# Gate projection as extra columns of a two-pair v unit with tokens stationary, and matmuls on zeros at the start

## The chip, the cores and the metric

The kernel runs on one core of a Trainium2 chip. The metric is the device time of one execution in microseconds; lower is better. Five engines work side by side, each through its own queue in order: TensorE (PE, whose weight loads the profile lists as PEld), VectorE (DVE), ScalarE (ACT), GpSimd (POOL) and SyncE (SP), which here issues nearly all DMAs. Dependences between engines are semaphores, set by a tile framework.

## The reference

One layer of a bidirectional encoder over 1280 tokens (1024 of the prompt, 256 of the sample) of width 2048. Only the first line of matrix work is touched here: one projection of the normalised input onto all column groups, among them the values v of the attention, the values of the mLSTM, and 16 mLSTM gate columns.

```python
hn = rmsnorm(x, norm_w)
proj = jnp.einsum('btd,dp->btp', hn, w_in)
na_q, na_k, na_v, na_g, ml_qk, ml_v, ml_o, ml_z, ml_gp = jnp.split(proj, cuts, axis=-1)
att = neighbourhood_attention(...na_q, na_k, na_v...) * silu(na_g)
gates = ml_gp.reshape(B, T, 2, 2, ML_HEADS) + gate_b
h = rmsnorm(bidirectional_mlstm(mq, mk, mv, gates))
mem = h * sigmoid(ml_o) * silu(ml_z)
y = rmsnorm(x + concat(att, mem) @ w_out)
```

## The kernel before

Numbers are fp32; every matmul operand is split into a high part `hi` (a rounded copy, made by ACT) and a low part `lo` (source minus `hi`, made by DVE), and each product is the sum of three matmuls: hi·hi, hi·lo, lo·hi (`split`, `split_a`, L175 to L185).

The tokens are worked on in two groups. Group A is the first 768 tokens, group B the other 512. For group A the projection runs as 2x2x2 Strassen-Winograd: two halves of the tokens (384 each), two halves of K (1024 each) and two halves of a pair of column blocks (128 columns each), so that 7 products stand for 8. The seven x operands, already summed and split, lie in SBUF for the whole phase (`xop`, L278; product 1 reads `xb`, the others `xg`). `first_tiles` (L294) builds them while it does the first four column blocks without Strassen: for each K block it loads x and weights, scales, splits and multiplies, and before its first matmul PE has nothing to do.

After that, `pair_a` (L479) does one pair of column blocks at a time, in an `order` (L615 to L618) of 34 pairs. It reads the pair's weights in four rounds of 512 KB (`ra` buffers, three of them), POOL makes the four weight sums of products 5, 6, 7 and 3 (`wt` tiles, `NWT` = 4 buffers), each of seven sources is split into a `wsa` tile (8 buffers), and PE takes the weights as the stationary and the 384 tokens as the moving operand: 168 matmuls of 384 columns for a pair. The seven products accumulate in seven of the eight PSUM banks (tags `pr` with 3 and `a` with 5) and are added up by DVE in `fold` in the last round. What remains of a pair, `finish_a` (L434), is a generator `bg`, whose steps are issued between the products of the next pair. For ten pairs (`SECOND`, L39) the four weight sums are also stored to DRAM (`sD`, L547) for group B, so a `wt` buffer is free only when that store has landed.

The v pairs (numbers `NCH` = 56 and up, eight of them) come out of this with columns on the partitions, and `finish_a` turns them by 12 PE transposes per pair (L470) before they are split (L177, L178, through `vo` tiles) and stored to `vS`. Group B's v projection, `proj_v` (L738), instead has the tokens stationary and 256 weight columns moving, and needs no transposes; in its unit 4 it appends the 16 gate columns (272 moving).

For group A the gate columns are a separate step, `gates_a` (L567), issued once behind the second pair (pair 6): it splits four sets of gate weights, runs 64 matmuls of 384 columns with the gate weights stationary (L591), and 12 small ones (L599) that add the two parts and turn the result into `gt`, the gate tile with tokens on the partitions.

`pc` tiles (5 buffers of 768 columns) hold results of pairs and the pieces of their finish. Tile tags and buffer counts are fixed; the framework's scheduler orders the instructions of each engine by its own simulated time line, with `tc.issue_after` pinning some of them. A v projection's weights lie in `w_in` as rows of 1024 numbers per K block pair, laid out by `_layout` (L1786).

Of the kernel before, what the change touches and what calls it, by code (L numbers as in the profile page):

```python
# [29 lines left out]
NRA, NWS, NWT, NPC, NPO = 3, 8, 4, 5, 6  # L30
# [5 lines left out]
LAG = 2  # L36
XFIRST = (0, 1, 8, 9, 2, 3, 10, 11, 4, 5)
# [10 lines left out]
def kernel(  # L48
# [242 lines left out]
    def wsa(name):  # L291
        return wa.tile([P, 2, 256], F32R, tag="wsa", name=name, bufs=NWS)

    def first_tiles():  # L294
# [41 lines left out]
        S.mul(mhalf[:, 15:16], ones[:, 0:1], 1.0)  # L336
        for kk in range(8):
# [96 lines left out]
    def finish_a(n1, Cn):  # L434
# [28 lines left out]
        if n1 >= NCH:  # L463
# [3 lines left out]
            for tt in range(GA // P):  # L467
# [3 lines left out]
                if tt in (1, 3):  # L471
                    vo = wa.tile([P, GA], F32R, tag="pc", name=f"{nm}vo{tt}", bufs=NPC)
                    vo = vo[:, :512].rearrange("p (a d) -> p a d", a=2)
                else:
                    vo = wa.tile([P, 2, 256], F32R, tag="vo", name=f"{nm}vo{tt}", bufs=1)
                store_v((n1 - NCH) // 2, tt * P, vo, b[:, :256])
                yield

# [88 lines left out]
    def gates_a():  # L567
        raw = wa.tile([P, 1024], F32, tag="ra", name="gAw", bufs=NRA)
        DM.dma_start(raw[:, :256], w_g)
        ab = [raw[:, :P], raw[:, P : 2 * P]]  # L570
        ext = [raw[:, 256 : 256 + P], raw[:, 384 : 384 + P]]
        V.tensor_tensor(ext[0], ab[0], ab[1], op=ALU.add)
        V.tensor_scalar(ext[1], ab[0], -1.0, None, op0=ALU.mult)
        st = []
        for i, src in enumerate((*ab, *ext)):
            t = wsa(f"gAt{i}").rearrange("p h c -> p (h c)")[:, : 8 * 32 + 96]
            G.memset(f(t), 0.0)
            tv = t[:, :256].rearrange("p (k h c) -> p k h c", h=2, c=16)
            sv = src.rearrange("p (k c) -> p k c", c=16)
            split_a(tv[:, :, 0, :], tv[:, :, 1, :], sv)  # L580
            st.append(t)
        sel = raw[0:32, 512:528]
        V.tensor_tensor(sel, ident[0:32, 0:16], ident[0:32, 16:32], op=ALU.add)
        gs = pc("gAg")
        for th, prods in enumerate((((0, 1), (1, 2)), ((2, 3), (3, 7)))):
            b = bank("a", f"gAb{th}")[:, :HALF]
            n = 0
            for w_, i in prods:
                for kk in range(8):
                    for hl_ in range(2):  # L590
                        PE.matmul(  # L591
                            b, st[w_][:, kk * 32 : kk * 32 + P], xop(i, kk, hl_),
                            start=n == 0, stop=n == 31,
                        )
                        n += 1
            V.tensor_copy(gs[0:32, th * HALF : (th + 1) * HALF], b[0:32])
        for tt in range(GA // P):
            b = bank("a", f"gAt{tt}")
            PE.matmul(b[:, :16], gs[0:32, tt * P : (tt + 1) * P], sel, start=True, stop=True)  # L599
            V.scalar_tensor_tensor(  # L600
                gt[:, tt, :], b[:, :16], rcs[0][:, tt : tt + 1], gb_sb, op0=ALU.mult, op1=ALU.add
            )

# [12 lines left out]
    rest = list(range(KT0, QK0, 2)) + list(range(OT0, NCH, 2))  # L616
    for i in range(NU):
        order += [QK0 + 2 * i, NCH + 2 * i, *rest[2 * i : 2 * i + 2]]  # L618
# [8 lines left out]
    for i, n1 in enumerate(order):  # L627
        bg = pair_a(n1, bg, second_pools if i == len(order) - 1 else None, i == 0, i == 1)
        if i == 1:
            gates_a()  # L630
# [107 lines left out]
    def proj_v(u, X):  # L738
# [8 lines left out]
        for r in range(4):  # L747
            raw = w_piece(w_in[NCH // 2 + u, r], f"v{u}_{r}")
            rawv = raw.rearrange("p (j f q c) -> p f q j c", j=2, f=2, q=2)
# [1021 lines left out]
def _layout(inputs):  # L1771
# [16 lines left out]
    )  # L1788
    gorder = [d * 8 + w_ * 4 + h for w_ in range(2) for d in range(2) for h in range(4)]
# [67 lines left out]
```

## Time and profile before

| | us |
|---|---|
| median of 3 runs (2548.97 to 2551.59) | 2550.65 |
| the profiled execution, whole | 2547.7 |
| its span, first to last instruction | 2546.0 |
| start of the first real matmul in the span | 7.01 |
| start of pair 4, the first `pair_a` | 75.6 |
| start of the gate matmuls (L591) | 138.7 |
| start of pair 56, the first v pair | 181.2 |
| end of the last `pair_a` (pair 54) | 1096.4 |

The page gives busy time per engine over the span; windows give it for a stretch; the waits say who stood still for whom. In all of them `A56b` is a PSUM bank of pair 56, `A56s` its split weights, `A56t` its POOL sums, `A56r` its raw weights, `fb`, `fw`, `fx`, `xr` tiles of the opening, and a line number that of the listing above, where a helper such as `split_a` stands for all its callers. A merged row of the time line gives start, length, engine, line, operands and count. Matmuls overlap, so that a pitch, start to start, is shorter than the duration of one.

### The profile page before, as it was taken

What the parts mean: (1) busy time and instruction counts of PE and PEld (TensorE: products, weight loads), DVE (VectorE), ACT (ScalarE), POOL (GpSimd) and SP (SyncE); (2) the same over time, 40 slices, a digit from 0 to 9 for tenths busy, and PEclk for the clock granted to TensorE, in tenths of its full rate; (3) what the DMA queues carried; (4) which work ended last, traced back from release to release, by engine and by line L of the source; (5) the groups of instructions that cost most, each with busy time, mean ns of one, the idle gap of its engine ahead of it and who ended that gap; (6) DMA issues with size and microseconds to landing.
All of it is one profiled execution on the core that took longest, in us unless ns stands there. A gap on an engine that the chain in (4) does not pass through costs nothing.

```text
span 2546.0 us, 44819 instructions
## 1 busy us (share of the span) xinstructions
PE 2527.1 (99%) x15150; PEld 2368.1 (93%) x15150; DVE 1979.3 (78%) x4049; ACT 1348.3 (53%) x3053; POOL 604.2 (24%) x895
## 2 busy tenths in 40 slices
PE   8999999999999999999999999999999999999998
PEld 8999999999999999999999899899998888888887
DVE  8768888898869798988875686776775665889696
ACT  8635545444444444465655666566665553344445
POOL 0435545444444444410000011010100103000002
PEclk9999999999999999999999999999999999999999
DMA  6556474536434343476777889888877849646227
GB/s 216 159 160 197 146 231 133 185 120 189 129 118 129 105 128 100 137 246 210 232 249 265 265 276 289 271 260 273 300 225 242 287 129 353 203 147 211 89 87 256
DMA packets 307757, 505.67 MB, mean 199 GB/s; under 512 B 48992, under 2 KB 195080, under 8 KB 307528
## 3 DMA queue, kind: packets, MB, share of 16 engines
q1 hardware_dynamic: 304424, 490.75, 59.9%
q0 software_dynamic: 2960, 11.80, 1.2%
q8 instruction: 120, 1.97, 0.3%
q14 instruction: 109, 0.89, 0.1%
q10 hardware_dynamic: 144, 0.26, 0.0%
HBM read 374.18 MB, written 128.52 MB: 197 GB/s over the span
## 4 chain that ended last, share of the span: by engine, by line
PE 85%; DMA 1%; DVE 0%; issue 0%; SPq 0%; ACT 0%; POOLq 0%; POOL 0%; ACTq 0%
PE pc L686 16%; PE po L1676 15%; PE pv L769 7%; PE A16b L286 1%; PE A40b L286 1%; PE A52b L286 1%; PE A48b L286 1%; PE A44b L286 1%; PE A20b L286 1%; PE A54b L286 1%; PE A14b L286 1%; PE A46b L286 1%; PE A22b L286 1%; PE A70b L286 1%; PE A38b L286 1%; PE A50b L286 1%
## 5 line engine op out<-in xcount | busy, mean ns | idle before, releaser
L1676 PE MATMUL po<-wo,mo 128*128 128x512 f32 (+1 forms) x1620 | 374.2, 392 | 0.0
L1676 PEld LDWEIGHTS po<-wo,mo 128*128 128x128 f32 x1620 | 303.4, 188 | 70.1
L178 DVE TENSOR_TENSOR ws<-wr,ws 128x512 fp32r<-128x512 f32 x144 | 98.2, 691 | 39.9 <-ACT ws L177 39.4
L177 ACT CAST ws<-wr 128x512 fp32r<-128x512 f32 x144 | 87.5, 617 | 66.4 <-PE pc L686 55.0
L177 ACT CAST mo<-mb 128x640 fp32r<-128x640 f32 x72 | 52.0, 726 | 111.6 <-PE po L1676 100.8
L118 POOL TENSOR_SCALAR rs<-rs 128x1 f32<-128x1 f32 x9 | 4.2, 468 | 369.8 <-DVE rs L1629 366.7
L178 DVE TENSOR_TENSOR mo<-mb,mo 128x640 fp32r<-128x640 f32 x72 | 58.6, 819 | 30.5 <-ACT mo L177 30.4
L1597 DVE TENSOR_TENSOR y<-y,po 128x512 f32<-128x512 f32 x89 | 57.1, 679 | 13.9 <-PE po L1676 13.8
L177 ACT CAST mo<-ms 128x640 fp32r<-128x640 f32 x40 | 28.9, 725 | 50.6 <-PE po L1676 32.7
L178 DVE TENSOR_TENSOR wsv<-wr_v,wsv 128x512 fp32r<-128x512 f32 x64 | 43.9, 692 | 13.3 <-ACT wsv L177 13.0
L177 ACT CAST wsv<-wr_v 128x512 fp32r<-128x512 f32 x64 | 38.9, 617 | 24.2 <-PE pv L769 12.7
L424 DVE SCALAR_TENSOR_TENSOR pcv<-pco,cw_sb,pcv 128x516 f32<-128x516 f32 x48 | 36.6, 763 | 8.8 <-ACT pcv L418 8.7
L178 DVE TENSOR_TENSOR mo<-ms,mo 128x640 fp32r<-128x640 f32 x40 | 32.7, 816 | 10.2 <-ACT mo L177 10.2
L1110 POOL MEMSET mls_0v<- 128x2 f32 x4 | 0.4, 102 | 162.8 <-DVE S_dt.float L178 137.4
L131 ACT ACTIVATE xq<-xq 128x1024 f32<-128x1024 f32 x20 | 21.2, 1060 | 31.5 <-DMA xq<-in_xtok_dram 31.5
L1611 ACT ACTIVATE jk<-y 128x512 f32<-128x512 f32 x39 | 24.5, 629 | 25.2 <-DVE y L1597 24.9
L286 PE MATMUL fb<-xg,fw 128*128 128x384 f32 x192 | 34.5, 334 | 0.0
L286 PEld LDWEIGHTS fb<-xg,fw 128*128 128x128 f32 x192 | 33.4, 188 | 0.0
L1560 DVE TENSOR_TENSOR ms<-mb,mb 128x640 f32<-128x640 f32 x40 | 32.6, 815 | 0.0
L807 DVE CUSTOM_DVE_ANT_0 nap_0st<-nap_0s,nap_0bt 128x384 f32<-128x384 f32 x32 | 17.7, 552 | 19.0 <-PE nap_0s L802 7.4
L263 DVE TENSOR_TENSOR pco<-pc,rstdb 128x512 f32<-128x512 f32 x28 | 19.1, 686 | 16.3 <-PE pc L686 16.1
L286 PE MATMUL fb<-xb,fw 128*128 128x384 f32 x96 | 23.7, 353 | 7.0 <-ACT fw L184 7.0
(2787 smaller groups left out, 8515.0 us busy)
## 6 DMA issues: line engine op xcount, KB each, us to landing
wr<-in_w_in_dram SPq DMA_DIRECT2D x72, 512.0 KB, 4.8
wr_v<-in_w_in_dram SPq DMA_DIRECT2D x32, 512.0 KB, 4.9
wb<-in_w_o_dram SPq DMA_DIRECT2D x48, 256.0 KB, 3.4
xq<-in_xtok_dram SPq DMA_DIRECT2D x20, 512.0 KB, 4.7
mb<-mx POOLq DMA_DIRECT2D x32, 320.0 KB, 7.9
y<-in_xtok_dram SPq DMA_DIRECT2D x35, 256.0 KB, 5.4
wr_wp<-in_w_o_dram SPq DMA_DIRECT2D x16, 512.0 KB, 6.7
vS<-vo SPq DMA_DIRECT2D x24, 256.0 KB, 5.1
```

Source lines behind the costliest of these rows:

```text
L131: S.activation(raw, raw, AF.Square, accum_out=ssq[g][:, t, q : q + 1])
L177: S.copy(hi, src)
L178: return V.tensor_tensor(lo, src, f(hi), op=ALU.subtract)
L263: V.tensor_tensor(o, src, rb, op=ALU.mult)
L286: PE.matmul(o, w(a_), x(b_), start=first and m == 0, stop=last and m == 2)
L424: V.scalar_tensor_tensor(dst[:, a:n], src[:, a + j - pad : n + j - pad], cw_sb[:, ct, j : j + 1], dst[:, a:n], op0=ALU.mult, op1=ALU.add,)
L686: PE.matmul(pb[j], t[j][:, wi, c : c + P], xs[xi], start=first and m == 0, stop=last and m == 2,)
L769: PE.matmul(outs[tt], xs[:, tt * P : (tt + 1) * P], t[:, wi, q * w : (q + 1) * w], start=first and m == 0 and (gates or tt % 2 == 0), stop ...
L1560: V.tensor_tensor(t, x, y_, op=op)
L1597: V.tensor_tensor(Y[p, q, tt], Y[p, q, tt], bk, op=op)
L1611: S.activation(jk, Y[p, q, tt], AF.Square, accum_out=ss[t][:, c : c + 1])
L1676: PE.matmul(bk[tt] if o is None else o, m[xi][:, tt * P : (tt + 1) * P], w[wi][:, cs], start=first and kk == 0 and j == 0, stop=last and j ...
```

## The change

The first two v pairs (56 and 58) are no longer two calls of `pair_a` but one `unit_v`, which computes 4 column blocks (512 columns) with the same seven products, x (128 tokens at a time) stationary and 256 weight columns moving. Products 1, 2, 3 and 7 get the 16 gate columns appended (272 moving); `gates_a` is removed, and `gt` is filled from the last columns of these products. 7 products x 3 token tiles x 256 columns do not fit into PSUM at once, so the unit makes three passes over K: products 1, 7, 5, then 6 and 3, then 2 and 4. Passes 1 and 2 load all of the unit's weights per K block (`whole`, rows of 256 numbers), pass 3 its second K half alone. Gated weights lie in `wide` tiles: tag `pc`, or tag `vo` with one buffer of 544 columns. Results are kept in four `pc` tiles and stored by `finish_v` without transposes, scaled by `rcs` in the split.

`NWT` falls from 4 to 3 buffers. The pair `OT0` (40) moves ahead of the unit, so that `order` becomes 4, 6, 24, 40, unit, 8, 26, 10, 12, 28, 60 and so on. The weights of the unit's two v blocks get another column order in DRAM, and `proj_v` reads it so for `u < 2`. In `first_tiles`, 15 matmuls of 384 columns on a zeroed tile go ahead of the first real matmul, into the bank `pb[7]`, which the first real matmul there overwrites.

```diff
-NRA, NWS, NWT, NPC, NPO = 3, 8, 4, 5, 6
+NRA, NWS, NWT, NPC, NPO = 3, 8, 3, 5, 6
+WARM = 15
...
         S.mul(mhalf[:, 15:16], ones[:, 0:1], 1.0)
+        idle = pc("idle")[:, :HALF].bitcast(F32R)
+        V.memset(f(idle), 0.0)
+        for i in range(WARM):
+            PE.matmul(pb[7], idle[:, :P], idle, start=True, stop=True)
...
+    def wide(name, i):
+        if i % 2:
+            return wa.tile([P, GA], F32R, tag="pc", name=name, bufs=NPC)[:, :544]
+        return wa.tile([P, 544], F32R, tag="vo", name=name, bufs=1)
+
+    def finish_v(u, z, C):
+        for tt in range(3):
+            t = 3 * z + tt
+            vo = wide(f"V{u}o{t}", tt % 2)[:, :512].rearrange("p (a d) -> p a d", a=2)
+            store_v(u, t * P, vo, C[:, tt * 256 : (tt + 1) * 256], rcs[0][:, t : t + 1])
+            yield
...
+    def unit_v(u, bg, gw):
...
+        def weights(i, kk, src):
+            gated = i in (1, 2, 3, 7)
+            if gated:
+                t = wide(f"{nm}s{kk}{i}", i == 1 or i in (2, 3) and kk % 2 == 0)
+                t = t.rearrange("p (h c) -> p h c", h=2)
+            else:
+                t = wsa(f"{nm}s{kk}{i}")
+            hi = S.copy(t[:, 0, :256], src)
+            lo = V.tensor_tensor(t[:, 1, :256], src, f(t[:, 0, :256]), op=ALU.subtract)
+            last_split["ins"] = lo.ins
+            if gated:
+                with tc.issue_after(hi.ins), tc.issue_after(lo.ins):
+                    split(t[:, 0, 256:], t[:, 1, 256:], gw[:, i == 2, kk], -1.0 if i == 7 else None)
+            splits[i, kk] = t, hi.ins, lo.ins
+
+        def multiply(i, kk, b):
+            t = splits[i, kk][0]
+            w = 272 if i in (1, 2, 3, 7) else 256
+            for tt, (o, own, closes) in enumerate(b[i][0]):
+                for m, (xi, wi) in enumerate(((0, 0), (0, 1), (1, 0))):
+                    PE.matmul(
+                        o, xop(i, kk, xi)[:, tt * P : (tt + 1) * P], t[:, wi, :w],
+                        start=kk == 0 and own and m == 0, stop=kk == 7 and closes and m == 2,
+                    )
...
+        def source(i, kk, A, src):
+            if i == 1:
+                return A[0, 0]
+            t = wa.tile([P, 256], F32, tag="wt", name=f"{nm}t{kk}{i}", bufs=NWT)
+            if i == 5:
+                G.tensor_tensor(t, A[1, 0], A[1, 1], op=ALU.add)
+            elif i == 6:
+                G.tensor_tensor(t, src[5], A[0, 0], op=ALU.subtract)
+            elif i == 7:
+                G.tensor_tensor(t, A[0, 0], A[1, 0], op=ALU.subtract)
+            elif i == 3:
+                V.tensor_tensor(t, A[0, 1], src[6], op=ALU.subtract)
+            return t
...
+        def first(i, kk, b):
+            if kk < 7:
+                if i in (5, 7):
+                    next(bg, None)
+            elif i == 1:
...
+                for c, o in b[1][1]:
+                    S.copy(C[0][:, c], o)
+                gate(1, b)
+            elif i == 7:
+                new(2)
+                gate(7, b)
+                plus(2, 0, 7, b)
+            else:
+                new(3)
+                new(1)
+                plus(3, 2, 5, b)
+                plus(1, 0, 5, b)
...
+        def second(i, kk, b):
+            if kk == 7 and i == 6:
+                for h in range(2):
+                    for q in (1, 2, 3):
+                        plus(q, q, 6, b, slice(h, h + 1))
+            elif kk == 7:
+                gate(3, b)
+                plus(1, 1, 3, b)
+                scaled_gates(1)
+
+        def third(i, kk, b):
+            if kk == 7:
+                if i == 2:
+                    gate(2, b)
+                    scaled_gates(0)
+                plus(i - 2, i - 2, i, b)
+
+        def steps():
+            b = {1: place(1, ("pr",) * 3), 7: place(7, ("a",) * 3), 5: place(5, "a", "a")}
+            for kk in range(8):
+                A = whole(kk, "r")
+                for i in (1, 7, 5):
+                    yield i, kk, b, source(i, kk, A, None), first
+            b = {6: place(6, "pr", "a"), 3: place(3, ("pr", "pr", "a"))}
...
+            b = {2: place(2, ("a",) * 3), 4: place(4, "pr", "a")}
...
+        for step in chain(steps(), (None,)):
+            if step is not None:
+                weights(step[0], step[1], step[3])
+            if todo is not None:
+                i, kk, b, _, after = todo
+                multiply(i, kk, b)
+                with ExitStack() as es:
+                    if step is not None and kk == 7:
+                        for ins in splits[step[0], step[1]][1:]:
+                            es.enter_context(tc.issue_after(ins))
+                    after(i, kk, b)
+            todo = step
+        return chain(*(finish_v(u + q // 2, q % 2, C[q]) for q in (1, 3, 0, 2)))
...
-    def gates_a():
...
+        if n1 == NCH:
+            bg = unit_v(0, bg, gw)
+        else:
+            bg = pair_a(n1, bg, second_pools if i == len(order) - 1 else None, i == 0, i == 1)
         if i == 1:
-            gates_a()
+            gw = wa.tile([P, 2, 8, 16], F32, tag="gw", name="gw", bufs=1)
+            DM.dma_start(gw, w_g.rearrange("p (f k c) -> p f k c", f=2, c=16))
...
+            if u < 2:
+                rawv = raw.rearrange("p (f q j c) -> p f q j c", f=2, q=2, j=2)
+            else:
+                rawv = raw.rearrange("p (j f q c) -> p f q j c", j=2, f=2, q=2)
...
+    vw = w_in[NCH // 2 : NCH // 2 + 2].reshape(2, 4, P, 2, 2, 2, P).transpose(0, 1, 2, 4, 5, 3, 6)
+    w_in[NCH // 2 : NCH // 2 + 2] = vw.reshape(2, 4, P, 1024)
```

More of the change, by code (lines that the diff above doesn't have):

```diff
@@ L565, in pair_a @@
         return finish_a(n1, Cn)
-    def gates_a():
[L568 to L602, printed above, removed]
     opening = first_tiles()
```

74 lines of the change are left out of this document (68 added, 6 removed).

## The prediction

> **What bounds the kernel now.** First the head of the page and the windows of the two halves: TensorE (PE) is busy nearly all the time.
>
> ```profile
> span 2546.0 us, 44819 instructions
> PE 2527.1 (99%) x15150; PEld 2368.1 (93%) x15150; DVE 1979.3 (78%) x4049; ACT 1348.3 (53%) x3053; POOL 604.2 (24%) x895
> 40.00:1096.00 1056.00, 1054.09 (x6092) 1048.61 (x6091) 881.63 (x1599) 517.94 (x1230) 492.10 (x552) 1.00 0.48 150
> PE fb L286 <- ACT fw L184: 7.0, 1, 7.0
> PE A4b L286 <- DVE A4s L185: 0.8, 3, 0.3
> ```
>
> In a window's row the length comes first, then busy time and count of PE, PEld, DVE, ACT and POOL, then clock and DMA share. From 40 to 1096 us, where the change lies, PE idles 1.9 us of 1056, and the waits (last two rows: total, times, longest) hold only the 7.0 us before the first matmul and trifles. So in this part time is the sum of PE's matmul pitches; whatever leaves PE is saved, as long as the other engines keep up.
>
> Next the places that the diff touches: a v pair (A56), the pair behind a v pair, in which its 12 transposes run (A40), one with neither (A10), the gate matmuls (three windows), and the two pairs around them.
>
> ```profile
> 181.21:210.31 29.10, 29.10 (x169) 29.10 (x169) 28.81 (x46) 15.15 (x35) 15.03 (x15) 1.00 0.40 119
> 682.87:713.27 30.40, 30.40 (x180) 30.23 (x180) 26.22 (x51) 13.65 (x36) 14.49 (x18) 1.00 0.41 138
> 240.80:270.10 29.30, 29.30 (x171) 29.26 (x170) 22.95 (x45) 14.67 (x36) 18.05 (x16) 1.00 0.72 230
> 138.72:149.96 11.24, 11.24 (x66) 10.99 (x65) 7.60 (x17) 3.28 (x8) 2.75 (x4) 1.00 0.51 141
> 149.96:150.72 0.76, 0.76 (x7) 0.73 (x6) 0.66 (x3) 0.41 (x1) 0.00 (x0) 1.00 1.08 344
> 154.27:155.04 0.77, 0.77 (x7) 0.74 (x7) 0.34 (x2) 0.34 (x1) 0.71 (x1) 1.00 0.61 189
> 108.80:138.72 29.92, 29.57 (x169) 29.11 (x169) 26.85 (x55) 17.18 (x43) 14.68 (x19) 1.00 0.71 209
> 150.72:181.20 30.48, 30.48 (x175) 30.20 (x175) 17.56 (x40) 11.35 (x28) 11.06 (x15) 1.00 0.47 140
> ```
>
> **Removed: the gate matmuls.** 64 matmuls of 384 columns and 12 small ones took 11.24 + 0.76 + 0.77 = 12.77 us of PE. Upper bound: the pairs around them last 29.92 and 30.48 - 0.77 = 29.71 against 29.10, so up to 1.43 us more may hang on the gates. I take 12.8; the neighbours have other reasons too (the 0.8 us of waits at A4 are of this kind).
>
> **Two v pairs against one unit.** The two pairs cost 2 x 29.10 = 58.20 us for 336 matmuls of 384 columns (0.1732 each). The unit has 7 products x 8 K blocks x 3 token tiles x 3 hi/lo terms = 504 matmuls: 288 of 272 columns (products 1, 2, 3, 7) and 216 of 256. The second half's v projection already runs both widths, its x (tokens) stationary; its line alone gives:
>
> ```profile
> 1096.56:1100.28 3.72, 3.72 (x30) 3.72 (x31) 1.00 0.97 323
> 1837.41:1839.99 2.58, 2.58 (x22) 2.54 (x22) 1.00 1.01 371
> ```
>
> That is 0.1240 us for 272 columns and 0.1173 us for 256. The unit: 288 x 0.1240 + 216 x 0.1173 = 61.05 us, 2.85 more than the pairs, gates included. The weight loads, one for each matmul, are hidden at both pitches.
>
> The Trainium skill (TensorE: Matmul & The Clock Gate, "Back-to-back issue gap") gives sustained spacings of about 81 ns for 128 columns and 131 ns for 512, a large fixed part; an estimate on that line is 98 ns for 256, 100 for 272 and 114 for 384, hence 49.9 us for the unit against 38.4 for the pairs, 11.5 more instead of 2.85. This rule speaks against many short matmuls; the trace disagrees: from 256 to 384 columns the pitch grows by 56.0 ns of 173.2, so the fixed part is only 0.1173 - 2 x 0.0560 = 5 ns.
>
> **Removed: 24 transposes.** The trace shows two between matmuls:
>
> ```profile
> 692.22 0.38 PE L470 MATMUL A64v<-ident,A64c 128*128 128x128 f32 x2
> 692.36 4.79 PE L286 MATMUL A40b<-xg,A40s 128*128 128x384 f32 x26
> ```
>
> 0.14 us for two is 0.84 for 12, the lower bound; the pair with them lasts 30.40 - 29.30 = 1.10 us longer than A10, and 1.30 longer than A56, the upper bound. I take 1.1, as it holds the breaks around them: 2.2 us for both pairs (1.7 to 2.6).
>
> **Matmuls on zeros.** The first matmuls run slowly:
>
> ```profile
> 7.00:11.00 4.00, 3.99 (x12) 1.00 1.01 307
> 11.00:15.00 4.00, 4.00 (x24) 1.00 1.09 349
> 12.01 0.40 ACT L184 CAST fw<-fr 128x256 fp32r<-128x256 f32 x1
> 12.13 0.96 DVE L185 TENSOR_TENSOR xg<-xr,xg 128x768 fp32r<-128x768 f32 x1 [2.73 <-ACT xg L184]
> 13.12 0.68 PE L286 MATMUL fb<-xg,fw 128*128 128x384 f32 x3
> ```
>
> 12 in 4.00 us, then 24 in 4.00, though the clock column says 1.00 in both. 15 on zeros last 15 x 0.333 = 5.0 us; DVE and PE have nothing before 4.8 and 7.01 us, so they delay nothing. But the second half of the first K block starts at 13.12 and its operands are complete at 12.41 (ACT) and 13.09 (DVE). A faster first half can start it 0.7 us earlier at most, and then waits for DVE. I take 0.3 us (0 to 0.7).
>
> The Trainium skill (the same page, "What's actually happening") says that the array runs at half clock until some 3.4 us of activity; the doubling agrees. By this rule alone 12 slow matmuls would be worth 12 x 0.167 = 2.0 us, and the sum 1.7 us lower; it leaves out when the operands come.
>
> PE alone: -12.8 + 2.85 - 2.2 - 0.3 = **-12.4 us**.
>
> **What feeds the unit.** For each step ACT and DVE make a hi/lo split, as before (56 of them), plus 32 small ones for gate columns; POOL's 32 sums stay as many, and DVE gets 8 sums (product 3) that POOL made before.
>
> ```profile
> L185 DVE TENSOR_TENSOR A56s<-A56t,A56s 128x256 fp32r<-128x256 f32 x13 | 6.9, 537 | 0.0
> L185 DVE TENSOR_TENSOR A56s<-A56r,A56s 128x256 fp32r<-128x256 f32 x9 | 5.9, 654 | 0.0
> L185 DVE TENSOR_TENSOR A56s<-A56t,A56s x16: 408/412/959, 176.0 to 206.8; 128x256 fp32r<-128x256 f32 x16
> 152.21 0.23 DVE L600 SCALAR_TENSOR_TENSOR gt<-gAt,rstdc,gb_sb 128x16 f32<-128x16 f32 x1
> L1597 DVE TENSOR_TENSOR y<-y,po 128x512 f32<-128x512 f32 x89 | 57.1, 679 | 13.9 <-PE po L1676 13.8
> ```
>
> A split takes 0.412 us in the median, up to 0.959, and 0.585 on average here ((13 x 0.537 + 9 x 0.654) / 22). DVE's work in the unit: 56 x 0.585 + 32 x 0.23 + 8 x 0.585 = 44.8, and to empty PSUM 15 pieces of 256 columns (0.41), 6 of 512 (0.68) and 12 of 16 (0.23) = 13.0; in all 57.8 us under 61.05 of PE. DVE fits, with 3 us to spare, but the emptying comes in lumps. At the end of pass 1 the last product's four additions (2 x 0.68 + 2 x 0.41 = 2.2 us) have the next product's 9 x 0.117 = 1.06 to hide in: 1.1 us late, with product 3's sum and split queued behind them on DVE and PE waiting for these. At the end of pass 2 product 6's six additions take 3.3 us against 1.1: 2.2 us late if pass 3's first splits stand behind. Splits put ahead hide some of it: I take **+2.5 us** (0 to 3.3).
>
> **wt from 4 to 3 buffers.** POOL already waits here, for DVE's splits or, in the ten pairs that spill their sums, for the spill to land:
>
> ```profile
> POOL A10t L531 <- DMA sD<-A10t: 6.3, 3, 3.0
> DMA to landing us min/median/max: 2.1/3.6/4.6
> 260.83 0.43 DVE L185 TENSOR_TENSOR A10s<-A10r,A10s 128x256 fp32r<-128x256 f32 x1 [4.45 <-ACT A10s L184]
> L286 PE MATMUL A10b<-xb,A10s x24: 331/335/342, 240.8 to 263.7; 128*128 128x384 f32 x24
> ```
>
> A10's last round has its first split ready at 261.3 us and its first matmul (five pitches before 263.7) at 262.8: 1.5 us of cover in the worst spilling pair, up to eight splits of about 1 us elsewhere. With three buffers a sum waits for the spill one sum later, about 1 us. That stays under the cover: I take **+0.5 us**, with 0 and 10 x 1.1 = 11 as ends.
>
> The sum: -12.4 + 2.5 + 0.5 = -9.4, so 2547.7 - 9.4 = 2538.3 us for a run like the profiled one. The median shown (2550.65) is 2.95 above it: **2541 us**, with its own range 2538 to 2545.
>
> **Rivals.**
> (a) Nothing stalls and the upper bounds hold: -14.2 + 2.85 - 2.6 - 0.7 = -14.7, 2536 us. For it: eight splits of cover today and DVE below PE; against: passes that must empty banks.
> (b) The three wt buffers: each spilling pair loses 1.1 us: -12.4 + 2.5 + 11 = +1.1, 2552 us. For it: A10's 1.5 us of cover; against: it is the worst one.
> (c) The raw weights come too late. Passes 1 and 2 each read all 4 MB of the unit, pass 3 half, in rows of 1 KB where a pair reads 4 KB rows.
>
> ```profile
> A56r<-in_w_in_dram SPq DMA_DIRECT2D x4, 512.0 KB, 3.5
> fr<-in_w_in_dram SPq DMA_DIRECT2D x16, 256.0 KB, 6.3
> ```
>
> With the opening's 6.3 us (512-byte rows) and 3.5 us from landing to the last reader, three buffers give a K block per 9.8 / 3 = 3.27 us; pass 1 takes 3.4 on PE, pass 2 only 2.17: 8 x 1.1 = 8.8 us. -12.4 + 8.8 = -3.6, 2547 us. Against: at 3.5 us the ring gives 2.33.
> (d) Slower: DVE becomes the bound of the unit, every split at 0.959 as beside a running POOL sum: 64 x 0.959 + 7.4 + 13.0 = 81.8 us against 61.05, +20.7; -12.4 + 20.7 = +8.3, 2559 us. It decides from a mean split of 0.63 us on ((61.05 - 20.4) / 64); slower than before from 0.83. For it: 0.585 is near; against: that average already holds POOL's sums at the same rate.
> (e) The change does not do what it says: product 7's weights have a single buffer, so PE runs alone between refills. A refill (ACT 0.41, DVE up to 0.96, two small ones) is under the 2.17 us of the two products between; this would only add to (d).
>
> **How the numbers follow.** Forecast 0.50, (a) 0.24, (b) 0.08, (c) 0.08, (d) with (e) 0.10. A measurement tells 0.2%, 5.1 us, from no change: faster is below 2545.5, slower above 2555.8. Faster 0.50 + 0.24 + a quarter of (c) = 0.76; slower is (d), 0.10; the rest 0.14. The range reaches from below (a) to (b): 2534 to 2552; outside are (d), half of (b) and a little of (a).
>
> **What would show it.** The gate matmuls gone and the pairs around at 29.1 to 29.3 us; the unit's 504 matmuls within 61 us plus gaps; those gaps at its two pass ends, with DVE as releaser; full pitch from the first real matmul, but its second half still waiting for DVE near 13 us; spilling pairs no longer than 29.3. Wrong: gaps at every K block (DMA as releaser is (c), DVE with splits near 0.96 is (d)), or POOL waits on spills that reach PE (b).

## The result, and the profile after

| | before | after |
|---|---|---|
| median of 10 runs each, us | 2550.15 (2547.94 to 2551.59) | 2556.19 (2552.14 to 2559.32) |
| ratio, 95% interval | | 1.0022 [1.0014, 1.003] |
| profiled execution: span, granted clock | 2546.0, 0.999 | 2552.1, 0.998 |
| first half ends (last matmul of pair 54) | 1096.75 | 1102.85 |
| from there to the end of the span | 1449.25 | 1449.25 |

The changed kernel is slower, by 6 us or 0.22%: the wrong sign, and outside the range. In the two profiles the whole of it lies in the first half. The head of the page after says that PE has a little less work, although 5.1 us of matmuls on zeros are now in it, and that the time went into gaps:

```profile
span 2552.1 us, 45095 instructions
PE 2525.1 (99%) x15233; PEld 2362.4 (93%) x15233; DVE 1985.9 (78%) x4087; ACT 1346.7 (53%) x3088; POOL 595.4 (23%) x891
L534 PE MATMUL V0b<-V0s,xg 128*128 128x272 f32 (+1 forms) x360 | 54.3, 295 | 8.0 <-DVE A40c L679 3.8
```

PE's sum fell by 2.0 us (from 2527.1) and the span grew by 6.1. The costliest group that is new, the unit's matmuls on `xg`, stood still for 8.0 us. To find where, the first half is cut at the first matmul of each pair. The windows of the changed kernel for pair 6 (where the gates were), pair 24, the unit, and the two pairs behind it, 8 and 26:

```profile
107.10:137.00 29.90, 29.52 (x171) 29.17 (x170) 28.01 (x55) 17.89 (x43) 15.15 (x15) 1.00 0.78 233
137.00:166.10 29.10, 29.10 (x170) 29.10 (x169) 23.14 (x43) 12.93 (x33) 15.19 (x18) 1.00 0.59 182
195.20:269.70 74.50, 65.89 (x499) 63.33 (x498) 47.02 (x130) 28.30 (x99) 22.25 (x29) 0.98 0.51 162
269.70:301.40 31.70, 30.86 (x175) 30.15 (x176) 24.04 (x50) 15.97 (x42) 14.36 (x18) 1.00 0.76 218
301.40:334.40 33.00, 30.00 (x170) 29.13 (x170) 28.84 (x54) 17.16 (x42) 18.18 (x20) 1.00 0.64 196
```

The same cuts before gave 41.9 for pair 6, 30.5 for pair 24, 58.3 for the two v pairs, 30.5 for pair 8 and 29.1 for pair 26. So the 6.1 us are:

| where | before | after | difference |
|---|---|---|---|
| start of pair 4, and pair 4 | 75.6, 33.2 | 74.5, 32.6 | -1.7 |
| pair 6 and pair 24 (gates gone) | 72.4 | 59.0 | -13.4 |
| two v pairs, then the unit | 58.3 | 74.5 | +16.2 |
| pair 8 | 30.5 | 31.7 | +1.2 |
| pair 26 | 29.1 | 33.0 | +3.9 |
| all other pairs | | | -0.1 |

A few of the unit's last matmuls are issued behind the next pair's first one: pair 8's window shows x175 where a pair alone shows x169 to x171. With these five (0.12 us each) the unit takes 75.1 us and the two pairs behind it 64.1. By pitches alone it is 61.05 for the unit, and 29.3 + 29.1 = 58.4 for two such pairs: the unit lost 14.0 us, and the pairs behind it 5.7. Against the forecast sum of -9.4 the profiles show +6.1; of these 15.5 us, 11.5 lie in the unit (2.5 were allowed for) and 5.7 behind it, and the other terms give back about 2. In the unit's window DVE is busy for 47.02 of 74.50, ACT for 28.30, and POOL for 22.25: no engine is full. The waits of PE from 190 to 335 us (total, times, longest) name several releasers, none of them large:

```profile
PE V0b L534 <- DVE A40c L679: 3.8, 2, 2.0
PE V0b L534 <- ACT V0s L178: 2.8, 3, 1.4
PE A26b L287 <- DVE A8c L679: 2.6, 2, 1.5
PE A8b L287 <- ACT A8s L185: 1.3, 2, 0.7
PE V0b L534 <- ACT V0s L181: 0.6, 1, 0.6
PE V0b L534 <- DVE V0s L179: 0.5, 1, 0.5
PE A26b L287 <- DVE A26s L186: 0.4, 1, 0.4
PE V0b L534 <- DVE V0s L182: 0.4, 1, 0.4
```

The first is the unit's beginning. PE's time line there (start, length, operation, count, idle before it):

```profile
195.21 0.54 PE L534 MATMUL V0b<-V0s,xg 128*128 128x272 f32 x3
197.77 0.65 PE L534 MATMUL V0b<-V0s,xg 128*128 128x272 f32 x3 [2.02 <-DVE A40c L679]
200.15 0.64 PE L534 MATMUL V0b<-V0s,xg 128*128 128x272 f32 x3 [1.74 <-DVE A40c L679]
201.12 4.08 PE L534 MATMUL V0b<-V0s,xg 128*128 128x256 f32 x21
```

Three matmuls, a wait, three, a wait. The banks they need are those of pair 40, which DVE is still adding up. DVE's time line shows why it is late:

```profile
193.26 1.49 DVE L435 SCALAR_TENSOR_TENSOR A24cv<-A24c,A24cv 128x766 f32<-128x766 f32 x1
...
196.83 0.43 DVE L522 TENSOR_TENSOR V0s<-V0t,V0s 128x256 fp32r<-128x256 f32 x1 [1.28 <-ACT V0s L521]
197.17 1.60 DVE L679 TENSOR_TENSOR A40c<-A40c,A40b 128x384 f32<-128x384 f32 x3
198.69 0.95 DVE L182 SCALAR_TENSOR_TENSOR A24c<-A24cv,A24ch 128x766 f32<-128x766 f32 x1
199.55 1.01 DVE L679 TENSOR_TENSOR A40c<-A40c,A40b 128x384 f32<-128x384 f32 x2
```

Before and between the additions of pair 40 stands the finish of pair 24, a convolution with pieces of 1.49 and 0.95 us. The convolution is not alone there: ahead of the additions DVE also stood idle for 1.28 us, for ACT's half of one of the unit's own splits. ACT waited for POOL's sum, and POOL had waited 0.84 us for the piece of 1.49. An ordinary pair needs the last banks of its predecessor only from its fifth product on; the unit needs three `a` banks in its first steps. After the waits, 21 matmuls take 4.08 us, 0.19 each, and the next ones 0.117 again; windows of that stretch show what this is:

```profile
201.12:204.54 3.42, 3.42 (x19) 3.42 (x18) 3.42 (x12) 1.93 (x6) 0.00 (x0) 0.54 0.35 118
204.54:205.03 0.49, 0.49 (x6) 0.49 (x5) 0.05 (x1) 0.49 (x1) 0.00 (x0) 1.00 0.06 19
```

The granted clock fell to half for one stretch of 3.4 us, so the gaps cost 1.7 us a second time. The waits in the unit (8.0 us) and this make 9.7 of the 14.0; most of the rest lies in restarts behind the waits, 0.16 us each, and in pitches that are a little longer, which were not traced further.

Behind the unit its 12 finishing tiles go to DRAM. ACT's rows from the time line at its end and in pair 26:

```profile
264.55 1.06 ACT L132 ACTIVATE xq<-xq 128x1024 f32<-128x1024 f32 x1 [3.63 <-DMA xq<-in_xtok_dram]
...
303.58 0.51 ACT L181 ACTIVATE V0o<-V0c,rstdc 128x256 fp32r<-128x256 f32 x1 [3.44 <-DMA vS<-V0o]
```

ACT works in order. Here it stood 3.63 us for an x load of the second half, with the unit's last splits behind it (PE then waits 1.44 us), and 3.44 us for the store of an earlier `V0o` tile, since the `vo` tag has one buffer. DVE's half of that tile waits for ACT's with the additions of pair 8 behind it, and PE waits for those banks (`A8c`, 2.6 us in the list).

### The profile page after: what moved, and what is told of

Read it like the earlier page. It is cut to its first block, busy times and chain, and to the rows that moved or that the text cites. A ratio compares the mean times of both kernels' runs of the same rounds, so it can differ in the third digit from the quotient of the medians.

```text
span 2552.1 us, 45095 instructions
## 1 busy us (share of the span) xinstructions
PE 2525.1 (99%) x15233; PEld 2362.4 (93%) x15233; DVE 1985.9 (78%) x4087; ACT 1346.7 (53%) x3088; POOL 595.4 (23%) x891
## 4 chain that ended last, share of the span: by engine, by line
PE 80%; DMA 1%; DVE 0%; issue 0%; ACT 0%; POOL 0%; SPq 0%; POOLq 0%; DVEq 0%; ACTq 0%
PE pc L840 16%; PE po L1833 15%; PE pv L926 6%; PE A48b L287 1%; PE A52b L287 1%; PE A22b L287 1%; PE A18b L287 1%; PE A44b L287 1%; PE A46b L287 1%; PE A54b L287 1%; PE A50b L287 1%; PE A42b L287 1%; PE A70b L287 1%; PE A68b L287 1%; PE A34b L287 1%; PE A64b L287 1%
## 5 line engine op out<-in xcount | busy, mean ns | idle before, releaser
L179 DVE TENSOR_TENSOR mo<-mb,mo 128x640 fp32r<-128x640 f32 x72 | 58.7, 824 | 31.5 <-ACT mo L178 31.4
L534 PE MATMUL V0b<-V0s,xg 128*128 128x272 f32 (+1 forms) x360 | 54.3, 295 | 8.0 <-DVE A40c L679 3.8
L534 PEld LDWEIGHTS V0b<-V0s,xg 128*128 128x128 f32 x360 | 48.7, 195 | 10.4 <-DVE A40c L679 4.2
L287 PE MATMUL fb<-xg,fw 128*128 128x384 f32 x192 | 34.7, 335 | 0.7 <-ACT xg L185 0.7
```

What stands on the lines that cost most here:

```text
L179: return V.tensor_tensor(lo, src, f(hi), op=ALU.subtract)
L287: PE.matmul(o, w(a_), x(b_), start=first and m == 0, stop=last and m == 2)
L534: PE.matmul(o, xop(i, kk, xi)[:, tt * P : (tt + 1) * P], t[:, wi, :w], start=kk == 0 and own and m == 0, stop=kk == 7 and closes and m == 2,)
```

## The experiments

All ratios are to the kernel before on the same chip, with a 95% interval. Lengths of pairs come from one profile each. The opening up to the end of pair 4, whose instructions are the same in after, `a_order` and `a_plain`, took between 105.5 and 107.1 us in these three, so differences of single profiles under about 1.5 us are not read, unless they come back in several. A unit "with all its matmuls" is its length from its first matmul to the next pair's first, and 0.12 us more for each matmul that the next pair's window shows beyond 170; the next pair is shortened by as much.

**`b_warm`, `b_wt3`: the small parts alone.** The kernel before, with the matmuls on zeros, or with three `wt` buffers.

```diff
+        idle = pc("idle")[:, :HALF].bitcast(F32R)
+        V.memset(f(idle), 0.0)
+        for i in range(15):
+            PE.matmul(pb[7], idle[:, :P], idle, start=True, stop=True)
```

> The kernel before with the 15 matmuls on zeros alone. In the changed kernel the second half of the first K block starts 1.2 us earlier (11.90 against 13.12 us). If that is the matmuls' doing: first pair 1.1 us earlier (about 74.5 us instead of 75.6), time 1 us below before. If the earlier operands of that execution did it: within 0.3 us of before.

> The kernel before with three wt buffers instead of four, nothing else. Rival (the buffer count costs the ten spilling pairs): those pairs 1 us longer each, the whole +5 to +11 us. Main theory (the loss sits around the unit): every pair within 0.3 us of before, the whole within 2 us.

`b_warm`: 1.0001 [0.9992, 1.0011]; in its profile pair 4 starts at 75.2 (before 75.6) and ends at 107.3 (108.8), and the half ends at 1094.85 (1096.75). Pair 4 thus starts 0.4 us earlier, not the 1.1 expected. The 1.5 us at its end are at the edge of what is read here, and too little for ten runs to show. `b_wt3`: 0.9999 [0.999, 1.0008], and no pair from 6 on moved by more than 0.4 us. Going from four buffers to three costs nothing that these profiles show; rival (b) falls.

**`a_order`: another neighbour at the unit's start.** Pair 24, with its convolution, moves behind the unit.

```diff
-    order += [QK0, OT0, NCH, rest.pop(0), QK0 + 2, *rest[:2]]
+    order += [OT0, NCH, QK0, rest.pop(0), QK0 + 2, *rest[:2]]
```

> The changed kernel with the pair 24 (whose finish is the convolution) moved from two places ahead of the unit to right behind it: order 4, 6, 40, unit, 24, 8, 26. Main theory (the unit's start waits for VectorE's convolution work, which holds pc buffers and delays the emptying of pair 40's banks, and the gap costs the clock): the waits of 2.0 and 1.7 us at the unit's start and the stretch of half clock go, the unit is 6 to 8 us shorter (67 to 68 instead of 74.5), the whole 4 to 8 us faster than the changed kernel. Rival (the unit with its three passes loses this wherever it stands): unit still above 73 us, the whole within 2 us.

1.0043 [1.0028, 1.0058], 2558.79. Its windows of the unit and of pair 24 behind it:

```profile
164.70:231.10 66.40, 60.80 (x478) 58.83 (x478) 44.31 (x117) 24.31 (x88) 22.64 (x29) 1.00 0.51 157
231.10:266.30 35.20, 33.42 (x198) 32.50 (x197) 21.69 (x53) 15.61 (x44) 13.81 (x17) 1.00 0.72 209
```

With all its matmuls (28 of them late, 3.4 us) the unit takes 69.8 us, 5.3 less than in after, and no wait for pair 40's banks is left: the start, 3.8 us of waits and 1.7 of slow clock, was the neighbour's doing. But the three pairs behind now take 31.8, 34.7 and 32.7, and the half ends at 1102.85, just as in after: the whole was to be 4 to 8 us faster than after, and is not. The waits of ACT from 225 to 305 us say what they carry:

```profile
ACT V1o L181 <- DMA vS<-V0o: 7.0, 2, 5.1
ACT V0o L181 <- DMA vS<-V0o: 5.0, 2, 3.3
```

**`a_vo`: other tiles for the finish.** The 12 finishing tiles take split buffers instead of the one `vo` buffer and `pc`.

```diff
-            vo = wide(f"V{u}o{t}", tt % 2)[:, :512].rearrange("p (a d) -> p a d", a=2)
+            vo = wsa(f"V{u}o{t}")
```

> The changed kernel with the 12 finishing tiles of the unit taken from the eight split buffers instead of the one vo buffer and the pc buffers. Theory (pairs 8 and 26 are late because ScalarE stands before a finishing tile whose buffer still waits for its store, with the next splits behind it): pair 8 falls from 31.7 to below 30.3 us, pair 26 from 33.0 to 29.5, the whole 3 to 5 us faster. Rival (late weights and the three wt buffers delay them): both stay within 0.7 us, the whole within 1 us.

1.004 [1.0026, 1.0054]. Unit 75.4, pair 8 37.0, pair 26 29.5: pair 26 is cured and pair 8 pays, since its own splits now stand behind stores in the same buffers (one wait of PE for `A8s` of 4.3 us, and a slow stretch of the clock). Unit and both pairs are 141.9 us against 139.2.

**`a_half`, `a_xq`: thinner work around the unit.** `a_half` spreads the 12 tiles over pairs 8 and 26; `a_xq` moves the x loads five pairs later.

```diff
-        return chain(*(finish_v(u + q // 2, q % 2, C[q]) for q in (1, 3, 0, 2)))
+        return [chain(*(finish_v(u + q // 2, q % 2, C[q]) for q in qs)) for qs in ((1, 3), (0, 2))]
...
-        k = i - 4
+        k = i - 9
```

> The changed kernel with the unit's 12 finishing tiles in two parts: six behind the unit in pair 8, six in the pair after it (26), instead of all in pair 8. Theory (ScalarE stands before finishing tiles that wait for their stores, as they come twice as dense as behind one v pair): pairs 8 and 26 fall from 31.7 + 33.0 = 64.7 to 59 to 61 us, the whole 3 to 5 us below the changed kernel. Rival (the late raw weights of pair 8, behind the unit's own loads, make it): pair 8 still above 31 us and the sum above 63.

> The changed kernel with the eight loads and squares of x for group B five pairs later, away from the unit's end. Theory (at the unit's end ScalarE waits 3.6 us for such a load with the last pass's splits behind it): the 1.4 us wait of PE at 266 us goes, unit 1.5 to 3 us shorter, the whole 2 to 4 us faster. Rival (the last pass's own weights come late): the wait stays with the raw weights as what ScalarE waits for, the unit within 0.7 us of 74.5.

`a_half`: 1.0021 [1.0012, 1.0031], pairs 8 and 26 together 64.0 us instead of 64.7: the density of the finish is not what makes them slow. `a_xq`: 1.0017 [1.0007, 1.0026]; with all its matmuls the unit falls to 72.1, but pairs 8 and 26 are 32.2 and 33.6, and the three are 137.9 us against 139.2. More than half of what is saved in the unit comes back behind it.

**`a_plain`, `a_plain_half`: plain neighbours on both sides.** The order is written out so that the unit stands between pair 40 and pairs 42 and 44, which have no convolution and no stored sums; `a_plain_half` adds `a_half`'s edit and x loads four pairs later.

```diff
+    order = [
+        4, 6, 40, NCH, 42, 44, 24, 46, 8, 26, 48, 10, 28, 60, 12, 14, 30, 62, 16, 18,
+        32, 64, 20, 22, 34, 66, 50, 36, 68, 52, 38, 70, 54,
+    ]
```

> The changed kernel in another order of pairs: 4, 6, 40, unit, 42, 44, 24, 46, 8, 26, 48, 10 and so on, so that neither a convolution nor a pair that spills its sums stands next to the unit. Theory (the loss comes from what runs beside the unit's two ends): unit about 66 as with pair 24 behind it, the two pairs behind it below 31 us each, the end of this half 8 to 12 us earlier than in the changed kernel (1102.9), the whole 2 to 6 us faster than the kernel before. Rival (the twelve finishing tiles stall whatever is behind): the two pairs together still 3 us or more above 58.5.

> The order of a_plain with the finishing tiles in two parts and the loads of x for group B four pairs later. If the three causes add up: unit 63 to 65 us, the pairs behind it 29.1 to 29.6, the whole 5 to 10 us faster than the kernel before, which would leave of the forecast gain only the two pass ends. If only neighbours matter: the same as a_plain.

`a_plain`: 1.0002 [0.9993, 1.0012], the half ends at 1092.25, 10.6 us earlier than in after. With all its matmuls the unit takes 71.5, and the pairs behind it 29.7 and 30.3. `a_plain_half`: 0.9993 [0.9983, 1.0003], unit 72.7, then 29.5 and 29.1. So the neighbours make the loss behind the unit, which is gone, and some 3 us of that in it; 10 us in the unit stay, where 66 us for `a_plain` and 63 to 65 for `a_plain_half` had been expected. PE's largest waits in `a_plain` from 160 to 345 us:

```profile
PE V0b L534 <- ACT V0s L178: 2.9, 1, 2.9
PE V0b L534 <- DVE V0s L179: 1.3, 1, 1.3
PE V0b L534 <- DVE V0c L565: 1.0, 1, 1.0
```

Lines 178 and 179 are the gate columns of the splits: gated weights, which live in `vo` and `pc`.

**`a_gwwt`, `a_vo2`, `a_defer`: what feeds the unit.** `a_gwwt` gives back the fourth `wt` buffer, in which the gate weights lie until the unit is done, so that it helps behind the unit alone. `a_vo2` gives gated weights a second `vo` buffer, and takes one of the eight split buffers to make room. `a_defer` issues the additions that end product 5 and product 6 one product later, which are the lumps of the prediction; in it, and in `a_best`, product 3's first K block takes gate weights before they are summed, so gate values differ and the work is the same.

```diff
-        return wa.tile([P, 544], F32R, tag="vo", name=name, bufs=1)
+        return wa.tile([P, 544], F32R, tag="vo", name=name, bufs=2)
...
-                    after(i, kk, b)
+                    for later in held:
+                        later()
+                    held.clear()
+                    if kk == 7 and i in (5, 6):
+                        held.append(lambda i=i, b=b, after=after: after(i, 7, b))
+                    else:
+                        after(i, kk, b)
```

> The changed kernel with four wt buffers (the gate weights lie in one of them until the unit is done). Rival (beside the unit's finish the third buffer is missed, since pair 8 spills its sums): pairs 8 and 26 together below 62 us instead of 64.7, the whole 2 us or more faster. Main theory (ScalarE and VectorE stand before finishing tiles and late evictions): the sum within 1 us of 64.7, the whole within 1.5 us of the changed kernel.

> The changed kernel with two vo buffers instead of one, paid for with one split buffer less (7). Theory (the single vo buffer makes each finishing tile wait for the store of the last but one): pairs 8 and 26 together 61 to 63 us instead of 64.7, product 7 and 2 no longer the first to wait in the unit; the whole 2 to 4 us faster. Rival (the waits are for pc buffers, raw weights or VectorE): the sum within 1 us, the whole within 1.5 us, or slower by the missing split buffer.

> The changed kernel with the additions of product 5 (end of pass 1) and product 6 (end of pass 2) issued one product later, behind the splits of the product after next. Theory (VectorE's lumps of 2.2 and 3.3 us at the pass ends keep the next splits waiting): the waits of PE at 227 to 233 us and 248 to 251 us (2.8 us together, and their drains) fall below 1 us, unit 2 to 4 us shorter, the whole as much faster. Rival (late raw weights or single buffers make these waits): unit within 1 us of 74.5.

`a_gwwt`: 1.0026 [1.0014, 1.0039], unit 74.5, pairs 8 and 26 64.7 together, all as in after. `a_vo2`: 1.0033 [1.0022, 1.0045], yet the unit with all its matmuls falls to 67.9, 7.2 less. Pairs 8 and 26, where this run was expected to gain, stay at 64.1, as in after, and the missing split buffer is paid in the opening (pair 4 starts at 76.2 and takes 36.3). `a_defer`: 1.0032 [1.0022, 1.0043], unit 78.0, mostly from longer waits and a longer slow stretch at its start. The wait of 0.6 us for `V0s` at L181, where the first pass ends, is unchanged, and all waits at the two pass ends come to 3.8 us, against 2.8 in after. The lumps of the prediction are not what PE waits for.

**`a_best`: several at once.** `a_plain_half` with `a_vo2`'s, `a_gwwt`'s and `a_defer`'s edits.

> The order of a_plain_half, its later loads of x and its divided finish, with the deferred additions, two vo and four wt buffers and 7 split buffers. If the causes are as the main theory has them: unit and pair 42 together 96 to 99 us (ideal 90.4, a_plain_half 102.2), no half clock, the whole 3 to 8 us faster than the kernel before. If the passes themselves cannot be fed: above 101 us and the whole within 2 us of before.

1.001 [1.0, 1.0019]. Unit 66.6 with all its matmuls and the pair behind it 29.5, as expected, but the whole is not faster: the opening with seven split buffers again loses: start 76.7, pair 4 35.0, pair 6 31.0.

**`a_vo2fix`: the second `vo` buffer without that price.** After, with `a_vo2`'s edit, where the opening and pairs 4 and 6 take some of their splits from `vo`, which is idle then.

```diff
-NRA, NWS, NWT, NPC, NPO = 3, 8, 3, 5, 6
+NRA, NWS, NWT, NPC, NPO = 3, 7, 3, 5, 6
...
-                    t = wsa(f"fw{kk}_{h}{g_}")
+                    if h and g_:
+                        t = wide(f"fw{kk}_{h}{g_}", 0)[:, :512].rearrange("p (h c) -> p h c", h=2)
+                    else:
+                        t = wsa(f"fw{kk}_{h}{g_}")
...
-                t = wsa(f"{nm}s{r}{i}")
+                if i == 3 and n1 in (4, 6):
+                    t = wide(f"{nm}s{r}{i}", 0)[:, :512].rearrange("p (h c) -> p h c", h=2)
+                else:
+                    t = wsa(f"{nm}s{r}{i}")
```

> The changed kernel with two vo buffers and 7 split buffers, where the opening and pairs 4 and 6 take one split in four or seven from the vo buffers, so that they have no fewer than before. Theory (the single vo buffer of product 7's weights starves the unit, and the missing split buffer cost the opening what was won): unit 65 to 67 us instead of 74.5, pair 4 starts at 74.5 to 75 and lasts 32 to 33, this half ends 5 to 8 us earlier than in the changed kernel (1102.9), the whole 4 to 8 us faster than it. Rival (the unit's shorter time in a_vo2 only moved waits into pairs 8 and 26): end of the half within 2 us of 1102.9.

With all its matmuls the unit takes 67.8, and pairs 8 and 26 32.2 and 31.9: together 131.9 against 139.2 in after, all of the 7.3 us in the unit. Some 1.5 us of them are at its start, where the waits for pair 40's banks fall from 3.8 to 2.3 us. The half ends 4.3 us earlier, at 1098.55. The whole, which was to be 4 to 8 us faster than after, does not show it: 1.0029 [1.0019, 1.0039], 2556.43. PE's time line inside the unit, first pass and then third:

```profile
214.99 1.29 PE L537 MATMUL V0b<-V0s,xb 128*128 128x272 f32 x9
...
218.31 1.29 PE L537 MATMUL V0b<-V0s,xb 128*128 128x272 f32 x9
...
246.18 6.09 PE L537 MATMUL V0b<-V0s,xg 128*128 128x272 f32 x48
252.11 1.22 PE L537 MATMUL V0h<-V0s,xg 128*128 128x256 f32 x9
253.17 0.87 PE L537 MATMUL V0b<-V0s,xg 128*128 128x256 f32 x6
```

A K block of pass 1 takes 3.32 us, and the pitches make 18 x 0.1240 + 9 x 0.1173 = 3.29. In pass 3 PE takes 48 gated matmuls, more than five K blocks of product 2, in one go of 5.93 us. In after the same pass is broken by waits for the gate columns of the next split:

```profile
248.89 1.51 PE L534 MATMUL V0b<-V0s,xg 128*128 128x272 f32 x9 [0.57 <-ACT V0s L178]
251.15 3.82 PE L534 MATMUL V0b<-V0s,xg 128*128 128x272 f32 x30 [0.75 <-ACT V0s L178]
...
266.15 2.95 PE L534 MATMUL V0b<-V0s,xg 128*128 128x272 f32 x21 [1.44 <-ACT V0s L178]
```

ACT was late in both kernels, by as much and for the same reasons, raw rows and an x load. After, and then `a_vo2fix`, ACT's rows of that pass:

```profile
247.71 1.02 ACT L521 CAST V0s<-V0q 128x256 fp32r<-128x256 f32 x3 [1.32 <-DMA V0q<-in_w_in_dram]
249.97 1.02 ACT L521 CAST V0s<-V0q 128x256 fp32r<-128x256 f32 x3 [1.14 <-DMA V0q<-in_w_in_dram]
```

```profile
248.13 1.02 ACT L524 CAST V0s<-V0q 128x256 fp32r<-128x256 f32 x3 [1.05 <-DMA V0q<-in_w_in_dram]
251.09 0.71 ACT L524 CAST V0s<-V0q 128x256 fp32r<-128x256 f32 x2 [1.42 <-DMA V0q<-in_w_in_dram]
...
257.36 1.06 ACT L132 ACTIVATE xq<-xq 128x1024 f32<-128x1024 f32 x1 [4.29 <-DMA xq<-in_xtok_dram]
```

The x load kept ACT for 4.29 us here and for 3.63 in after. With a second buffer PE does not notice any of the three.

**`a_final`: both causes taken away.** `a_plain_half`'s order, divided finish and later x loads, with `a_vo2fix`'s buffers; every line of its diff is in the two above.

> Order, divided finish and later loads of x of a_plain_half with the vo buffers of a_vo2fix. If neighbours and vo buffer are the two causes: unit and pair 42 together 95 to 98 us (ideal 90.4), this half ends at 1086 to 1090 us (1096.7 before), the whole 4 to 9 us faster than the kernel before. Rival (something else in the unit's three passes costs the rest): above 100 us, the whole within 2 us of before.

2544.56 (2541.0 to 2546.06, 9 runs) against 2550.46: 0.9976 [0.9966, 0.9985], faster than both kernels. Its windows of the unit and of pairs 42 and 44, and the waits of PE from 163.7 to 290 us, all that the view lists:

```profile
168.30:231.10 62.80, 60.89 (x487) 59.65 (x487) 48.45 (x129) 25.52 (x94) 25.07 (x31) 1.00 0.57 174
231.10:262.80 31.70, 31.70 (x188) 31.70 (x187) 22.93 (x53) 15.20 (x39) 14.21 (x18) 1.00 0.61 164
262.80:291.90 29.10, 29.10 (x170) 29.10 (x169) 21.31 (x41) 13.48 (x32) 12.23 (x16) 1.00 0.46 141
```

```profile
PE V0b L537 <- DVE V0s L179: 1.2, 3, 0.8
PE V0b L537 <- DVE V0s L182: 0.6, 1, 0.6
```

With all its matmuls the unit takes 65.0 us, 3.9 over its pitches, at full clock, and pair 42 29.5: together 94.5, a little less than expected. The half ends at 1089.25, 7.5 us before the old kernel's. `a_plain_half`, from which this kernel differs by the buffers alone, has 72.7 for the unit, so the second `vo` buffer is worth as much (7.7 us, of which 3.4 are slow clock that `a_final` does not have) beside plain neighbours as in `a_vo2fix`.

## Why the prediction was wrong

**PE's own terms held.** The gates: -13.4 against -12.8, inside the two bounds. The unit's pitches: 48 gated matmuls in 5.93 us are 0.1235 each and the nine of 256 columns behind them 1.06 us, 0.118 each (`a_vo2fix`), against 0.1240 and 0.1173. The transposes: without a v pair ahead, pair 8 takes 29.4 us in `a_final` and 30.5 before, the 1.1 that was taken. Pair 12, which lost the second set, fell only from 30.9 to 30.3 in after; why was not traced.

**The zeros: the wait was misread, and what they are worth stays between 0.4 and 2 us.** The first matmuls after go at full pitch:

```profile
6.78:10.78 4.00, 4.00 (x23) 4.00 (x24) 1.50 (x4) 3.49 (x8) 0.00 (x0) 1.00 0.93 300
11.90 1.31 PE L287 MATMUL fb<-xg,fw 128*128 128x384 f32 x6 [0.67 <-ACT xg L185]
```

They are 23 in 4.00 us instead of 12, and the second half of the first K block starts at 11.90 after a wait for ACT's `xg`. The prediction went by other operands, complete at 12.41 and 13.09. In every profile with the zeros this half starts within 0.1 us of the end of ACT's `xg`. Before, that was written by 12.10, so those times allowed a gain of 1.0 us and not 0.7. In `b_warm`, where the zeros are the only edit, ACT's `xg` came later, and the gain is 0.65, inside the bound. The row of before, and then that of `b_warm`:

```profile
11.28 0.82 ACT L184 CAST xg<-xr 128x768 fp32r<-128x768 f32 x1
...
12.47 4.50 PE L286 MATMUL fb<-xg,fw 128*128 128x384 f32 x24 [1.39 <-ACT xg L184]
```

Pair 4 starts at 75.6 and 76.2 in the two profiles without zeros (before, `b_wt3`), at 75.2 in `b_warm`, and at 74.0 to 74.8 in the nine other kernels with zeros and eight split buffers. The profiles thus speak for more than the 0.3 us taken, but ten runs of `b_warm` show no gain.

**`wt`: +0.5 taken, 0 measured** (`b_wt3`, `a_gwwt`). The cover of 1.5 us in the worst pair may be why; that was not tested.

**The step that failed is "What feeds the unit".** It allowed 2.5 us, 3.3 at most; it came to 14.0 us in the unit and 5.7 behind it. It set DVE's work (57.8 us) against PE's (61.05) and looked for places where work comes in lumps. Both halves missed the loss. DVE was busy for 47.02 us, neighbours' work included, as a split took 0.48 us on average there (0.42 in the median) instead of the 0.585 taken, so rival (d) is not what happened. The waits at the ends of the passes came to 2.8 us, near the 2.5 taken, but that is luck: they did not go when the lumps were issued later (`a_defer`). Three things were there in its place, none of them a matter of how much work an engine has:

- The start. `a_order` and `a_plain` show it: with another neighbour no wait for pair 40's banks is left, and the unit is 5.3 and 3.6 us shorter (`a_plain` has a slow stretch of the clock in it, 1.7 us). The prediction counted the passes' own banks, and not when the unit needs those of the pair before it.
- The single `vo` buffer. Rival (e) named it and priced it at nothing, since a refill "is under the 2.17 us of the two products between". A refill is, when ACT and DVE are there at once. They are in-order queues that also carry finishes, x loads and additions, and with a single buffer PE has no product in hand while they are late. With two, the unit takes 67.9 and 67.8 us instead of 75.1 (`a_vo2`, `a_vo2fix`). Those kernels have seven split buffers for eight as well, which costs time in pair 4 (`a_vo2`) and was not tried without the other edit.
- The finish behind the unit. It was not costed at all: the prediction let the unit end at its last matmul. Its 12 tiles wait for stores in ACT's queue, a second `vo` buffer does not cure this (64.1 us for the two pairs in `a_vo2fix` as well), and the neighbours decide whether PE feels it: the two pairs behind the unit take 64.1 us in after and 58.6 in `a_plain_half`, against 58.4 by pitches.

The first two overlap: removed singly they are worth 5.3 (`a_order`) and 7.3 us (`a_vo2fix`) in the unit, and together, with the x loads moved away, 10.1 (`a_final`). The x loads alone are worth 3.0 (`a_xq`), while there is one `vo` buffer.

**The other rivals.** (a), nothing stalls, was not reached even by `a_final`, which has another order and other buffers: 2544.56, where the forecast was 2541 and (a) 2536. (c), raw weights too late, had a part in the third pass, where ACT's two waits for raw rows reach PE with 0.57 and 0.75 us, but only through the single buffer; and the K blocks of the second pass, where it put the loss, keep nearly their pitch, 2.27 us where 2.17 was computed and (c) had 3.27:

```profile
237.05:239.32 2.27, 2.27 (x21) 2.26 (x19) 2.26 (x6) 0.92 (x3) 1.77 (x2) 1.00 0.72 213
```

**What stays open.** Of the 3.0 us between `a_vo2fix`'s first half (-4.3) and its unit and pairs (-7.3), pair 4 (+1.2) and pair 12 (+1.3) hold most. The seven split buffers are likely: in the four kernels that have them pair 4 takes 33.8 to 36.3 us and pair 12 31.5 to 31.9, in the changed kernels with eight 31.4 to 32.6 and 29.5 to 30.8, but no run changes that alone. Why its whole is no faster than after is known only in part (see the last section). What the second `vo` buffer is worth with all eight split buffers wasn't tried, and `a_final`, with 34.2 us in pair 4, probably pays for the missing one too.

## What to carry to other kernels

A new stage isn't costed when its engines' work is shown to be less than the bound's: ask of every tile tag in it how many buffers it has, and what else stands in the queues that refill it, because with one buffer a late neighbour's work can reach the bounding engine. Look at what the stage needs from the one before it in its first steps, and at what it leaves for the one after it; here these two edges and one buffer turned a gain of about 6 us into a loss of 6. An order that puts plain stages at both edges is a cheap test of this.

## What the runs showed of the hardware

**A gap can be paid twice.** In after, PE is busy for 1.20 us of the 4.95 at the unit's start (window 195.20 to 200.15), and then the clock is halved for one stretch of 3.4 us, which costs 1.7 us, though groups of three matmuls stood between the gaps. Most of the variants had one or two such stretches in the first half, some of 6.8 us; in `a_final` and the profile of before it had none. But it does not always happen: in `a_plain` a stretch with PE busy for 1.17 us of 3.40 (window 214.80 to 218.20) was followed by half clock, and in `a_order` one with 1.20 of 3.40 (214.40 to 217.80) was not. The Trainium skill (TensorE: Matmul & The Clock Gate, "What's actually happening") gives a free-running window of about 3.4 us that decides between full and half clock. The length agrees with the 3.4 us seen here, and this trace adds that the window need not be empty.

```profile
195.20:200.15 4.95, 1.20 (x7) 0.75 (x6) 3.63 (x8) 1.63 (x5) 1.16 (x2) 1.00 0.20 79
```

**The same instructions do not always take the same time.** From the end of the first half to the end of the span these kernels have the same instructions, but for a few transposes of pair 70 (`a_plain`, `a_final`) and the column order of two v blocks' weights. There single profiles took 1449.25 us (before, after), 1454.15 (`b_warm`), 1454.85 (`a_plain`), 1455.05 (`a_final`) and 1455.85 (`a_vo2fix`). Most of it is waits of PE: they come to 1.5 and 1.6 us before and after, and to 4.6 to 6.3 in the other four. The longest single wait is for the load of `nap3qk`, 0.8 us before, 2.7 in `b_warm` and 2.4 in `a_vo2fix`. What makes these operands late was not traced. This is why the first half is used here to find places, and the medians to say what is faster.
